# The first gate/up blocks of a decoder layer: scale and shift moved to ScalarE, weight low parts moved to VectorE, another load order, seven conditioning rows moved

## The chip, the cores and the metric

The kernel runs on one core of a Trainium2 chip. The metric is the device time of one execution in microseconds (us), as the median over several runs. The core has five engines with queues of their own: TensorE (PE, with weight loads PEld), VectorE (DVE), ScalarE (ACT), GpSimd (POOL) and SyncE (SP, which issues the DMAs here). An engine takes its instructions strictly in the order of its queue; semaphores tie the queues together.

## The reference

One decoder layer on a sequence of 1024 rows of width 1024: a gated feed-forward net, a token mixer (a convolution branch and a windowed attention branch), a second feed-forward net, a final norm. All is float32. The change lies at the very start, in the first feed-forward net:

```
c_act = silu(c)
mods = c_act @ w_ada + b_ada          # 9 vectors of 1024: sh1, sc1, gt1, sh2, ...
h = rms_norm(x, g_ffn1) * (1 + sc1) + sh1
a, b = split(h @ w1_gu, 2)            # two times 2816 columns
x = x + 0.5 * gt1 * ((silu(a) * b) @ w1_down)
```

## The kernel before

Activations lie transposed: a tile holds 128 features (one of eight blocks `db`) by 512 rows of the sequence (half `h` 0 or 1). Float32 products are made of three matmuls in a rounded format: each operand is split into a high part (a cast) and a low part (the operand minus its high part), and wh·xh, wh·xl and wl·xh are summed in PSUM (`mm3`, L132; three matmuls, L138, L140, L142). A weight block `w1gu[j, i]` (j of 22 output blocks, i the gate or the up half) is loaded as one 128x1024 tile and split by halves of 512 columns (`split`, L105: the cast on ACT, L106; the subtraction, L107, on DVE or, here at the start, on POOL).

A "conditioning row" is one of the 72 blocks of 128 entries of `mods`: `ada_block` (L222) loads 128 rows of `w_ada` transposed and makes 128 dot products with silu(c) in one DVE instruction (L225). For the first norm, the rows m=0 (shift) and m=1 (scale) of each `db` are needed, 16 in all; `ada_done` (L229) turns the scale row into g·(1+sc), `amod`, on DVE (L235).

The first three output blocks (j = 0, 1, 2: six weight tiles, `w0[0]` to `w0[5]`) are worked on while the sixteen rows are still being made, one feature block after another, in an order written out by hand for DVE, ACT, SP and POOL (`manual_schedule`; PE is in hand order everywhere). For half 0: the sum of squares of x (`Stats`, L308: squares on ACT, L312 and L315, adds on DVE, L319; then four matmuls with a column of ones, L328, and a short chain on ACT and DVE, L253 to L260, `rstd`), spread over the partitions by four matmuls (L269) and copied to SBUF (`first_spread`, L640). Then eight times `first_step`, L665: DVE forms u = x·amod·spread (L275), ACT adds the shift and casts to the high part (L279), DVE makes a row of the next block, the low part (L290) and the other row, ACT writes the full value over x (L285). Between the steps stand `first_w` (two casts on ACT, two subtractions on POOL) and `first_mm`, the matmuls of the tiles whose weights are ready. The steps 6 and 7 are followed by the sum of squares of half 1, whose `rstd`, spread and `first_h` start the same work for half 1, with all six tiles ready.

Behind the hand order a planner takes over: it orders the later instructions of DVE, ACT, SP and POOL by its own estimate of times, and it may set a later instruction into the hand-ordered part where it expects an engine to be idle there. First behind the hand order come `all_seven` (sums and differences of the inputs for a seven-product scheme, L179 to L183), the products of blocks 0 to 2, `some_ada(7)` (seven conditioning rows of m=2), and `gu_seven` for the blocks 3 to 21 with one row for each block (`extra`). Weights and rows here go through one ring of four 128x1024 buffers (`load_st`, L112).

Of the kernel before, what the change touches and what calls it, by code (L numbers as in the profile page):

```python
# [10 lines left out]
AF = mybir.ActivationFunctionType  # L11
ALU = mybir.AluOpType

P = 128
# [21 lines left out]
def tile_macaron_layer(  # L36
# [36 lines left out]
    def bank():  # L73
        return ps.tile([P, 512], F32, tag="ps", name=nm("ps"), bufs=8)
# [4 lines left out]
    def tile_t(dt=F32R, shape=(P, 2, HALF)):  # L79
        return act.tile(list(shape), dt, tag="T", name=nm("t"), bufs=28)  # L80
# [4 lines left out]
    def scratch(tag, shape=(P, HALF)):  # L85
        return scr.tile(list(shape), F32, tag="r", name=nm(tag), bufs=8)
# [8 lines left out]
    def f32(t):  # L95
        return t.bitcast(F32)
# [4 lines left out]
    def pair_of(t):  # L101

        return t[:, 0, :], t[:, 1, :]

    def split(hi, lo, src, lo_engine=nc.vector):  # L105
        nc.scalar.copy(hi, src)  # L106
        lo_engine.tensor_tensor(lo, src, f32(hi), op=ALU.subtract)  # L107

    def parts_tile():
        return wgt.tile([P, 2, HALF], F32R, tag="w", name=nm("w"), bufs=8)  # L110

    def load_st(src):  # L112
        st = wgt.tile([P, 1024], F32, tag="wr", name=nm("wr"), bufs=4)
        nc.sync.dma_start(st[:, : src.shape[1]], src)
        return st

    class Weights:


        def __init__(self, raw, n=1024, lo_engine=nc.vector, tiles=None):  # L120
            self.half = m = n // 2
            self.t = tiles or [parts_tile() for _ in range(2)]
            for i in range(2):
                hi, lo = pair_of(self.t[i])
                split(hi[:, :m], lo[:, :m], raw[:, i * m : (i + 1) * m], lo_engine)

        def __call__(self, c0, n=P):
            i, c = c0 // self.half, c0 % self.half
            return self.t[i][:, 0, c : c + n], self.t[i][:, 1, c : c + n]

    def load_w(src, lo_engine=nc.vector, tiles=None):
        return Weights(load_st(src), src.shape[1], lo_engine, tiles)  # L132

    def mm3(outs, w, xs, start, stop):

        wh, wl = w
        for o, (xh, xl) in zip(outs, xs):
            mm(o, wh, xh, start=start, stop=False)  # L138
        for o, (xh, xl) in zip(outs, xs):
            mm(o, wh, xl, start=False, stop=False)  # L140
        for o, (xh, xl) in zip(outs, xs):
            mm(o, wl, xh, start=False, stop=stop)  # L142
# [130 lines left out]
    def modulated_hi(xsrc, pb, which, db, hi):  # L273
        u = scratch("u")
        nc.vector.scalar_tensor_tensor(  # L275
            out=u, in0=xsrc, scalar=amod[:, which * 8 + db : which * 8 + db + 1], in1=pb,
            op0=ALU.mult, op1=ALU.mult,
        )
        nc.scalar.activation(  # L279
            hi, u, AF.Identity, bias=mods[:, which * 24 + db : which * 24 + db + 1]  # L280
        )
        return u

    def modulated_full(u, which, db, dst):
# [193 lines left out]
    def gu_seven(wgu, js, hid, ts, extra=lambda to: None):  # L478

        seven_stream([(wgu[j, 0], wgu[j, 1], GateValue(hid, j)) for j in js], ts, extra)  # L480
# [151 lines left out]
    with tc.tile_pool(name="f1", bufs=2) as tmp:  # L632
# [3 lines left out]
        def load_x(h):  # L636
            for db in range(KT):
                nc.sync.dma_start(xT[db][h], x_block(db, h))

        def first_spread(rr):  # L640
            sp = scratch("spr")
            nc.scalar.copy(sp, spread(rr))
            return sp

        def first_h(dbs, h):
            us = [modulated_hi(xT[db][h], sp, 0, db, hh[db][h]) for db in dbs]
            for u, db in zip(us, dbs):
                modulated_lo(u, 0, db, hh[db][h], hl[db][h])
            for u, db in zip(us, dbs):
                modulated_full(u, 0, db, xT[db][h])  # L650

        def first_ada(db, m):
            ada_block(crow_act, m, db, sta.pop(0))
            if m == 1:
                ada_done(m, db, 1)

        def first_ada_load(db):
            for m in range(2):
                sta.append(tile_c(F32))
                nc.sync.dma_start(sta[-1], wada[m * 8 + db])  # L660

        def first_step(db):

            u = modulated_hi(xT[db][0], sp, 0, db, hh[db][0])
            if db + 1 < KT:  # L665
                first_ada(db + 1, 0)
            modulated_lo(u, 0, db, hh[db][0], hl[db][0])
            modulated_full(u, 0, db, xT[db][0])
            if db + 1 < KT:
                first_ada(db + 1, 1)  # L670

        def first_mm(dbs, h, which):
            for db in dbs:
                for i in which:
                    mm3([first[i, h]], w0[i](db * P),
                        [(hh[db][h], hl[db][h])], db == 0, db == KT - 1)

        def first_w(i):
            w0[i] = Weights(w0[i], 1024, nc.gpsimd, [tile_t(), tile_t()] if i > 3 else None)

        def first_sw(j, h):
            hid.put(j, h, swiglu_raw(first[2 * j, h], first[2 * j + 1, h], h == 0 or None))
# [6 lines left out]
        })  # L689
        order.__enter__()  # L690
        crow_act = tmp.tile([P, D], F32, tag="crow", name="crow_act", bufs=1)
        nc.sync.dma_start(crow_act, crow)
        nc.scalar.activation(crow_act, crow_act, AF.Silu)
        load_x(0)
        s0 = Stats(engine=nc.vector)
        for db in range(KT):
            s0.add(xT[db][0])
        sta, w0 = [], {}
        first_ada_load(0)
        w0[0] = load_st(w1gu[0, 0])  # L700
        w0[1] = load_st(w1gu[0, 1])
        first_ada_load(1)
        w0[2] = load_st(w1gu[1, 0])
        first_ada_load(2)
        w0[3] = load_st(w1gu[1, 1])
        first_ada_load(3)
        first_ada(0, 0)
        r0 = s0.rstd()
        first_ada(0, 1)
        first_w(0)  # L710
        w0[4] = load_st(w1gu[2, 0])
        sp = first_spread(r0)
        first_w(1)
        first = {(i, 0): bank() for i in range(6)}
        first_ada_load(4)
        first_step(0)
        first_mm((0,), 0, (0, 1))
        first_w(2)
        first_ada_load(5)
        first_step(1)  # L720
        first_mm((1,), 0, (0, 1))
        first_mm((0, 1), 0, (2,))
        first_w(3)
        first_ada_load(6)
        first_step(2)
        first_mm((2,), 0, (0, 1, 2))
        first_mm((0, 1, 2), 0, (3,))
        first_w(4)
        first_ada_load(7)
        w0[5] = load_st(w1gu[2, 1])  # L730
        load_x(1)
        first_step(3)
        first_mm((3,), 0, (0, 1, 2, 3))
        first_mm((0, 1, 2, 3), 0, (4,))
        first_step(4)
        first_mm((4,), 0, (0, 1, 2, 3, 4))
        first_step(5)
        first_mm((5,), 0, (0, 1, 2, 3, 4))
        first_w(5)
        s1 = Stats(engine=nc.vector)  # L740
        first_step(6)
        for db in range(2):
            s1.add(xT[db][1])
        first_mm((6,), 0, (0, 1, 2, 3, 4))
        first_step(7)
        for db in range(2, KT):
            s1.add(xT[db][1])
        first_mm((7,), 0, (0, 1, 2, 3, 4))
        r1 = s1.rstd()
        first_sw(0, 0)  # L750
        first_mm((0, 1, 2), 0, (5,))
        sp = first_spread(r1)
        first_mm((3, 4, 5, 6, 7), 0, (5,))
        first.update({(i, 1): bank() for i in range(6)})
        steps = [(m, k) for m in range(2, 9) for k in range(KT)]

        def some_ada(n):
            for _ in range(n):
                if steps:
                    ada_step(crow_act, *steps.pop(0))  # L760
# [11 lines left out]
        ts = all_seven(tt, xT)  # L772
        for j in range(3):
            first_sw(j, 1)
        some_ada(7)
        gu_seven(w1gu, range(3, NJ), hid, ts, lambda to: some_ada(1))

        gate, ngate = gates_of(2)
        xT = by_half(tile_x)
# [626 lines left out]
```

## Time and profile before

| | us |
|---|---|
| median of three runs | 2294.13 (2292.82 to 2300.34) |
| the profiled execution | 2291.84 |
| its span, first to last instruction | 2289.7 |
| PE busy in the span | 2206.0 (96%) |
| DVE busy | 1675.7 (73%) |
| ACT busy | 1061.9 (46%) |
| POOL busy | 395.0 (17%) |

The span is the time between the first and the last instruction on the chip; what lies around it, 2.1 us, is start and end of the program. A row of the timeline gives the start of an instruction, its duration, its engine and line, and in brackets how long the engine had been idle before it and what released it. "x8" is a run of eight instructions of one kind in one row. L269 and L328 show two PE instructions for one matmul of the program. A duration is longer than the distance to the next instruction, since instructions overlap in an engine's pipeline; where instructions follow each other, the distance of the starts is what one costs.

### The profile page before, as it was taken

What the parts mean: (1) busy time and instruction counts of PE and PEld (TensorE: products, weight loads), DVE (VectorE), ACT (ScalarE), POOL (GpSimd) and SP (SyncE); (2) the same over time, 40 slices, a digit from 0 to 9 for tenths busy, and PEclk for the clock granted to TensorE, in tenths of its full rate; (3) what the DMA queues carried; (4) which work ended last, traced back from release to release, by engine and by line L of the source; (5) the groups of instructions that cost most, each with busy time, mean ns of one, the idle gap of its engine ahead of it and who ended that gap; (6) DMA issues with size and microseconds to landing.
All of it is one profiled execution on the core that took longest, in us unless ns stands there. A gap on an engine that the chain in (4) does not pass through costs nothing.

```text
span 2289.7 us, 30099 instructions
## 1 busy us (share of the span) xinstructions
PE 2206.0 (96%) x10392; PEld 1845.3 (81%) x10392; DVE 1675.7 (73%) x2966; ACT 1061.9 (46%) x2095; POOL 395.0 (17%) x445
## 2 busy tenths in 40 slices
PE   5899999999998999999899997999999999999997
PEld 3688888888887888888889996788888888888786
DVE  8897778767868777777477776554786776676876
ACT  4554444444446443343476555123644444454443
POOL 3000000006452000000344443002100000002644
PEclk9899999999999999999999998999999999999998
DMA  8265456599732543444121115454233553389932
GB/s 322 74 221 172 149 185 212 181 406 299 270 115 106 184 134 107 155 157 155 56 64 57 49 48 212 133 170 155 75 120 120 184 184 120 120 326 343 337 116 74
DMA packets 146744, 381.63 MB, mean 167 GB/s; under 512 B 20384, under 2 KB 22560, under 8 KB 146592
## 3 DMA queue, kind: packets, MB, share of 16 engines
q1 hardware_dynamic: 141984, 371.33, 46.5%
q0 software_dynamic: 4608, 8.39, 2.1%
q8 instruction: 81, 1.33, 0.2%
q14 instruction: 71, 0.58, 0.1%
HBM read 270.61 MB, written 109.05 MB: 166 GB/s over the span
## 4 chain that ended last, share of the span: by engine, by line
PE 86%; DVE 7%; issue 2%; ACT 1%; DMA 1%; POOL 1%; SPq 0%; POOLq 0%; DVEq 0%; ACTq 0%
PE ps L195 60%; PE ps L142 6%; PE ps L140 6%; PE ps L138 6%; PE ps L977 2%; PE ps L975 2%; PE ps L976 2%; DVE w L107 1%; PE ps L1031 1%; PE ps L1074 1%; DVE t L225 1%; DMA wr<-in_w2d_dram 1%; POOL s L319 1%; PE ps L1010 1%; PE ps L1098 1%
## 5 line engine op out<-in xcount | busy, mean ns | idle before, releaser
L195 PE MATMUL ps<-t,w 128*128 128x512 f32 x6468 | 1469.2, 389 | 5.0 <-DVE r L405 3.0
L195 PEld LDWEIGHTS ps<-t,w 128*128 128x128 f32 x6468 | 1213.4, 188 | 260.4 <-DVE r L405 5.8
L106 ACT CAST w<-wr 128x512 fp32r<-128x512 f32 (+1 forms) x420 | 255.3, 613 | 481.2 <-PE ps L195 365.3
L107 DVE TENSOR_TENSOR w<-wr,w 128x512 fp32r<-128x512 f32 (+1 forms) x404 | 304.4, 760 | 137.8 <-ACT w L106 136.2
L515 POOL TENSOR_TENSOR x<-x,g 128x512 f32<-128x512 f32 x96 | 145.2, 1526 | 1061.5 <-DMA t<-hs 941.1
L106 ACT CAST w<-ws 128x512 fp32r<-128x512 f32 x231 | 143.9, 623 | 250.3 <-PE ps L195 200.6
L140 PE MATMUL ps<-t,w 128*128 128x512 f32 (+1 forms) x528 | 204.9, 388 | 6.5 <-DVE t L290 6.5
L107 DVE TENSOR_TENSOR w<-ws,w 128x512 fp32r<-128x512 f32 x231 | 161.4, 703 | 39.4 <-ACT w L106 39.0
L138 PE MATMUL ps<-t,w 128*128 128x512 f32 (+1 forms) x400 | 156.2, 390 | 7.2 <-ACT t L279 7.2
L142 PE MATMUL ps<-t,w 128*128 128x512 f32 (+1 forms) x400 | 154.4, 386 | 1.1 <-DVE w L107 1.1
L140 PEld LDWEIGHTS ps<-t,w 128*128 128x128 f32 x528 | 100.4, 190 | 28.4 <-DVE t L290 9.2
L344 DVE TENSOR_TENSOR x<-x,x 128x512 fp32r<-128x512 f32 x161 | 102.8, 687 | 2.9 <-ACT x L343 2.8
L343 ACT CAST x<-x 128x512 fp32r<-128x512 f32 x161 | 88.8, 624 | 20.4 <-DVE x L431 10.2
L225 DVE CUSTOM_DVE_ANT_0 wr<-wr,crow_act,v 128x1024 f32<-128x1024 f32 x56 | 71.7, 1282 | 36.0 <-DMA wr<-in_wada_dram 35.9
L138 PEld LDWEIGHTS ps<-t,w 128*128 128x128 f32 x400 | 76.4, 191 | 23.9 <-ACT t L279 9.8
L569 DVE SCALAR_TENSOR_TENSOR x<-ps,mods,x 128x512 f32<-128x512 f32 (+1 forms) x104 | 72.9, 706 | 23.6 <-PE ps L195 12.9
L107 POOL TENSOR_TENSOR w<-wr,w 128x512 fp32r<-128x512 f32 (+1 forms) x16 | 21.5, 1358 | 397.3 <-ACT w L106 397.3
L142 PEld LDWEIGHTS ps<-t,w 128*128 128x128 f32 x400 | 76.4, 191 | 16.5 <-DVE w L107 1.8
L319 POOL TENSOR_TENSOR s<-s,q 128x512 f32<-128x512 f32 (+1 forms) x48 | 56.8, 1185 | 188.8 <-ACT q L315 187.3
L975 PE MATMUL ps<-w,t 128*128 128x384 f32 x256 | 88.3, 345 | 0.0
L977 PE MATMUL ps<-w,t 128*128 128x384 f32 x256 | 85.7, 335 | 0.0
L976 PE MATMUL ps<-w,t 128*128 128x384 f32 x256 | 85.6, 335 | 0.0
(150 smaller groups left out, 2815.6 us busy)
## 6 DMA issues: line engine op xcount, KB each, us to landing
t<-hs SPq DMA_DIRECT2D x140, 512.0 KB, 9.9
hs<-x SPq DMA_DIRECT2D x277, 256.0 KB, 4.6
wr<-in_wada_dram SPq DMA_DIRECT2D x56, 512.0 KB, 3.8
wr<-in_w1gu_dram SPq DMA_DIRECT2D x44, 512.0 KB, 4.6
wr<-in_w2gu_dram SPq DMA_DIRECT2D x44, 512.0 KB, 3.6
wr<-in_wbcu_dram SPq DMA_DIRECT2D x24, 512.0 KB, 4.1
wr<-in_w1d_dram SPq DMA_DIRECT2D x22, 512.0 KB, 7.5
wr<-in_w2d_dram SPq DMA_DIRECT2D x22, 512.0 KB, 7.5
```

Of the source, the lines that this page charges most:

```text
L106: nc.scalar.copy(hi, src)
L107: lo_engine.tensor_tensor(lo, src, f32(hi), op=ALU.subtract)
L138: mm(o, wh, xh, start=start, stop=False)
L140: mm(o, wh, xl, start=False, stop=False)
L142: mm(o, wl, xh, start=False, stop=stop)
L195: mm(o, a, b, start=first, stop=last, skip_group_check=True)
L225: nc.vector.tensor_tensor_reduce(out=st, in0=st, in1=crow_act, scale=1.0, scalar=v[:, C_BADA + i : C_BADA + i + 1], op0=ALU.mult, op1=ALU. ...
L344: nc.vector.tensor_tensor(f32r(t), t, f32(hi), op=ALU.subtract)
L515: nc.gpsimd.tensor_tensor(dst, dst, r, op=ALU.add)
L975: mm(o[:, :384], xh, wh, start=k == 0, stop=False)
L976: mm(o[:, :384], xh, wl, start=False, stop=False)
L977: mm(o[:, :384], xl, wh, start=False, stop=k == KT - 1)
```

## The change

In the hand-ordered part:

1. x of half 0 is loaded ahead of the broadcast c (`crow`), and silu(c) stands behind the squares of x on ACT.
2. `amod` is now 1+sc, made on ACT. u is x·g·spread and doesn't depend on the conditioning any more. ACT applies scale and shift and writes the high part and the full value, one right behind the other. The low part is the full value minus the high part, a plain subtraction on DVE, behind both rows of the next block.
3. The spread for half 0 is read by DVE from PSUM, without the copy. Twelve small matmuls that nobody reads (`keep_busy`) stand on PE ahead of it, eight behind it.
4. The weight tiles are split half by half (`LateWeights.make`), with the subtraction on DVE in place of POOL, at places listed in `plan`; the matmuls of a step are issued as all high ones (`first_mm_hi`), then all low ones (`first_mm_lo`), then the tiles that are caught up (`late`).
5. The loads of the rows, of x of half 1 and of the last two weight tiles stand at other places of SP's order. The sum of squares of half 1 is spread over the steps 4 to 7.
6. `some_ada(7)` goes; the blocks 10 to 17 of `gu_seven` take two rows each instead of one.

```diff
+        def make(self, i):
+            split(*pair_of(self.t[i]), self.raw[:, i * HALF : (i + 1) * HALF])
...
+        def first_u(db, h):
+            u = scratch("u")
+            nc.vector.scalar_tensor_tensor(
+                out=u, in0=xT[db][h], scalar=v[:, C_G1 + db : C_G1 + db + 1], in1=sp,
+                op0=ALU.mult, op1=ALU.mult,
+            )
+            return u
+        def first_hi(u, db, h):
+            for dst in (hh[db][h], xT[db][h]):
+                nc.scalar.activation(
+                    dst, u, AF.Identity, bias=mods[:, db : db + 1],
+                    scale=amod[:, db : db + 1],
+                )
+        def first_lo(db, h):
+            nc.vector.tensor_tensor(
+                hl[db][h], xT[db][h], f32(hh[db][h]), op=ALU.subtract)
...
         def first_ada(db, m):
             ada_block(crow_act, m, db, sta.pop(0))
             if m == 1:
-                ada_done(m, db, 1)
+                nc.scalar.activation(
+                    amod[:, db : db + 1], mods[:, 8 + db : 9 + db], AF.Identity, bias=ones)
...
+        def keep_busy(n):
+            o = bank()
+            for _ in range(n):
+                mm(o[:, 0:P], ident, ident, start=True, stop=True)
...
+        load_x(0)
         nc.sync.dma_start(crow_act, crow)
-        nc.scalar.activation(crow_act, crow_act, AF.Silu)
-        load_x(0)
         s0 = Stats(engine=nc.vector)
         for db in range(KT):
             s0.add(xT[db][0])
+        nc.scalar.activation(crow_act, crow_act, AF.Silu)
...
         first_ada(0, 0)
+        first_ada(0, 1)
         r0 = s0.rstd()
-        first_ada(0, 1)
...
+        keep_busy(12)
+        first_ada(1, 0)
+        sp = spread(r0)
+        keep_busy(8)
+        first_ada_load(5)
+        load_x(1)
+        first_ada_load(6)
+        first_ada_load(7)
...
+        plan = (
+            ([(0, 0), (1, 0)], (0, 1), ()),
+            ([(2, 0)], (0, 1), [((0, 1), (2,))]),
+            ([(3, 0)], (0, 1, 2), [((0, 1, 2), (3,))]),
+            ([(0, 1), (1, 1)], (0, 1, 2, 3), ()),
+            ([(2, 1)], (0, 1), [((4,), (2,))]),
+            ([(4, 0)], (0, 1, 2), [((0, 1, 2, 3), (4,))]),
+            ([(3, 1)], (0, 1, 2), [((4, 5, 6), (3,))]),
+            ([(4, 1), (5, 0), (5, 1)], (0, 1, 2, 3), [((4, 5, 6, 7), (4,))]),
+        )
+        for db, (pieces, which, late) in enumerate(plan):
+            first_hi(first_u(db, 0), db, 0)
+            for i, part in pieces:
+                if i > 3 and part == 0:
+                    w0[i] = load_st(w1gu[2, i - 4])
+                first_w(i, part)
+            first_mm_hi((db,), 0, which)
+            if db + 1 < KT:
+                if db:
+                    first_ada(db + 1, 0)
+                first_ada(db + 1, 1)
+            first_lo(db, 0)
+            first_mm_lo((db,), 0, which)
+            for dbs, tiles in late:
+                first_mm(dbs, 0, tiles)
+            if db >= 4:
+                for d in (2 * db - 8, 2 * db - 7):
+                    s1.add(xT[d][1])
         r1 = s1.rstd()
         first_sw(0, 0)
-        first_mm((0, 1, 2), 0, (5,))
+        first_mm((0, 1, 2, 3), 0, (5,))
         sp = first_spread(r1)
-        first_mm((3, 4, 5, 6, 7), 0, (5,))
+        first_mm((4, 5, 6, 7), 0, (5,))
...
-        some_ada(7)
-        gu_seven(w1gu, range(3, NJ), hid, ts, lambda to: some_ada(1))
+        gu_seven(w1gu, range(3, NJ), hid, ts,
+                 lambda to: some_ada(1 if to.j < 10 or to.j >= 18 else 2))
```

## Rows read from the trace of the kernel before

**Rows 1.** Busy time of the engines in three stretches of the first 115 us. Columns: stretch, its length, then busy us and instructions of PE, PEld, DVE, ACT, POOL, the granted clock, the DMA share, GB/s.
```profile
20.00:40.00 20.00, 11.73 (x33) 7.80 (x34) 19.71 (x22) 8.08 (x15) 14.10 (x8) 1.00 1.03 407
60.00:80.00 20.00, 11.13 (x40) 8.71 (x39) 16.12 (x30) 6.15 (x11) 0.00 (x0) 0.68 0.55 184
100.00:115.00 15.00, 15.00 (x68) 12.43 (x67) 15.00 (x26) 7.71 (x15) 0.00 (x0) 1.00 0.12 35
```

**Rows 2.** Who waited for whom before 85 us: the waiting engine and line, the releaser, us in total, times, the longest.
```profile
PE ps L328 <- DVE s L319: 21.8, 2, 13.2
PE ps L138 <- ACT t L279: 7.2, 5, 2.4
PE ps L140 <- DVE t L290: 4.7, 6, 2.2
```

**Rows 3.** The timeline of DVE between the last low part and the sum of squares of half 1: the first of the seven rows of m=2, and the last add.
```profile
60.97 1.28 DVE L225 CUSTOM_DVE_ANT_0 wr<-wr,crow_act,v 128x1024 f32<-128x1024 f32 x1
...
72.42 0.69 DVE L319 TENSOR_TENSOR s<-s,q 128x512 f32<-128x512 f32 x1
```

**Rows 4.** The timeline of DVE in the steps: u of the first step, u of the third, one whole step, and a run of plain subtractions later on.
```profile
20.08 0.75 DVE L275 SCALAR_TENSOR_TENSOR u<-x,amod,spr 128x512 f32<-128x512 f32 x1 [0.37 <-ACT spr L642]
...
33.10 1.75 DVE L275 SCALAR_TENSOR_TENSOR u<-x,amod,spr 128x512 f32<-128x512 f32 x1
...
44.15 0.75 DVE L275 SCALAR_TENSOR_TENSOR u<-x,amod,spr 128x512 f32<-128x512 f32 x1
44.82 1.28 DVE L225 CUSTOM_DVE_ANT_0 t<-t,crow_act,v 128x1024 f32<-128x1024 f32 x1
...
46.02 0.75 DVE L290 SCALAR_TENSOR_TENSOR t<-u,mods,t 128x512 fp32r<-128x512 f32 x1
...
48.21 0.75 DVE L275 SCALAR_TENSOR_TENSOR u<-x,amod,spr 128x512 f32<-128x512 f32 x1
...
100.31 1.89 DVE L107 TENSOR_TENSOR t<-x,t 128x512 fp32r<-128x512 f32 x3
```

**Rows 5.** The timeline of ACT: the high part, the full value and two casts in the first step, the high part of the fifth, and the squares of half 1.
```profile
20.98 0.72 ACT L279 ACTIVATE t<-u,mods 128x512 fp32r<-128x512 f32 x1
21.61 0.71 ACT L285 ACTIVATE x<-u,mods 128x512 f32<-128x512 f32 x1
22.22 1.12 ACT L106 CAST w<-wr 128x512 fp32r<-128x512 f32 x2
...
44.94 0.73 ACT L279 ACTIVATE t<-u,mods 128x512 fp32r<-128x512 f32 x1 [2.72 <-DVE u L275]
...
60.78 3.23 ACT L315 ACTIVATE q<-x 128x512 f32<-128x512 f32 x6
```

**Rows 6.** The timeline of PE: the sum of squares and the spread of half 0, the same of half 1 with matmuls of the last tile around them, and the first matmul of half 1.
```profile
13.19 1.87 PE L328 MATMUL ps<-ones,s 128*128 128x1 f32 x8 [13.19 <-DVE s L319]
17.37 2.05 PE L269 MATMUL ps<-ident,nr 128*128 128x128 f32 x8 [2.32 <-DVE nr L260]
...
73.16 1.87 PE L328 MATMUL ps<-ones,s 128*128 128x1 f32 x8 [8.59 <-DVE s L319]
74.89 0.77 PE L138 MATMUL ps<-t,t 128*128 128x512 f32 x1
...
78.87 1.91 PE L269 MATMUL ps<-ident,nr 128*128 128x128 f32 x8
80.44 0.73 PE L138 MATMUL ps<-t,t 128*128 128x512 f32 x1
...
83.99 0.39 PE L142 MATMUL ps<-t,t 128*128 128x512 f32 x1
84.21 0.39 PE L138 MATMUL ps<-t,w 128*128 128x512 f32 x1
```

**Rows 7.** The timeline of ACT at the start, up to the square root of half 0.
```profile
4.79 1.06 ACT L693 ACTIVATE crow_act<-crow_act 128x1024 f32<-128x1024 f32 x1 [2.77 <-DMA crow_act<-in_crow_dram]
...
7.80 3.94 ACT L315 ACTIVATE q<-x 128x512 f32<-128x512 f32 x6 [0.40 <-DMA x<-in_x_dram]
11.75 1.28 ACT L253 ACT_TABLE_LOAD   x1
15.09 0.26 ACT L253 ACTIVATE nt<-ps,eps 128x4 f32<-128x4 f32 x1 [2.05 <-PE ps L328]
```

**Rows 8.** The timeline of PE at idle stretches later in the kernel.
```profile
688.42 1.05 PE L328 MATMUL ps<-ones,s 128*128 128x1 f32 x8 [0.30 <-POOL s L319]
693.43 1.16 PE L269 MATMUL ps<-ident,nr 128*128 128x128 f32 x8 [2.47 <-DVE nr L260]
1402.97 0.80 PE L138 MATMUL ps<-t,t 128*128 128x512 f32 x1 [5.44 <-ACT t L106]
```

**Rows 9.** Busy time of the engines in three stretches of 19 us, about one block of `gu_seven` each; columns as in rows 1.
```profile
269.00:288.00 19.00, 19.00 (x86) 15.73 (x85) 16.26 (x28) 10.41 (x19) 0.00 (x0) 1.00 0.60 201
288.00:307.00 19.00, 19.00 (x86) 15.73 (x85) 17.59 (x30) 10.41 (x19) 0.00 (x0) 1.00 0.79 273
307.00:326.00 19.00, 19.00 (x85) 15.75 (x84) 12.98 (x21) 7.08 (x12) 0.00 (x0) 1.00 0.47 162
```

More of the change, by code (lines that the diff above doesn't have):

```diff
@@ L129, in __call__, with __init__ @@
             return self.t[i][:, 0, c : c + n], self.t[i][:, 1, c : c + n]
+    class LateWeights(Weights):
+        def __init__(self, raw, tiles):
+            self.half, self.raw = HALF, raw
+            self.t = tiles or [parts_tile() for _ in range(2)]
+        def make(self, i):
+            split(*pair_of(self.t[i]), self.raw[:, i * HALF : (i + 1) * HALF])
     def load_w(src, lo_engine=nc.vector, tiles=None):
@@ L643, in first_spread @@
             return sp
+        def first_u(db, h):
[14 more added lines that the diff above has]
+                hl[db][h], xT[db][h], f32(hh[db][h]), op=ALU.subtract)
         def first_h(dbs, h):
-            us = [modulated_hi(xT[db][h], sp, 0, db, hh[db][h]) for db in dbs]
+            us = [first_u(db, h) for db in dbs]
             for u, db in zip(us, dbs):
-                modulated_lo(u, 0, db, hh[db][h], hl[db][h])
-            for u, db in zip(us, dbs):
-                modulated_full(u, 0, db, xT[db][h])
+                first_hi(u, db, h)
+            for db in dbs:
+                first_lo(db, h)
         def first_ada(db, m):
@@ L660, in first_ada_load, with first_mm_hi, first_mm_lo, first_w @@
                 nc.sync.dma_start(sta[-1], wada[m * 8 + db])
[L662 to L670, printed above, removed]
+        def first_mm_hi(dbs, h, which):
+            for db in dbs:
+                for i in which:
+                    wh, wl = w0[i](db * P)
+                    mm(first[i, h], wh, hh[db][h], start=db == 0, stop=False)
+                    mm(first[i, h], wl, hh[db][h], start=False, stop=False)
+        def first_mm_lo(dbs, h, which):
+            for db in dbs:
+                for i in which:
+                    mm(first[i, h], w0[i](db * P)[0], hl[db][h], start=False,
+                       stop=db == KT - 1)
         def first_mm(dbs, h, which):
             for db in dbs:
[L674 to L679, printed above, removed]
+                first_mm_hi((db,), h, which)
+                first_mm_lo((db,), h, which)
+        def keep_busy(n):
+            o = bank()
+            for _ in range(n):
+                mm(o[:, 0:P], ident, ident, start=True, stop=True)
+        def first_w(i, part):
+            if part == 0:
+                w0[i] = LateWeights(w0[i], [tile_t(), tile_t()] if i > 3 else None)
+            w0[i].make(part)
         def first_sw(j, h):
@@ L697, in tile_macaron_layer @@
             s0.add(xT[db][0])
+        nc.scalar.activation(crow_act, crow_act, AF.Silu)
         sta, w0 = [], {}
         first_ada_load(0)
+        first_ada_load(1)
         w0[0] = load_st(w1gu[0, 0])
         w0[1] = load_st(w1gu[0, 1])
-        first_ada_load(1)
+        first_ada_load(2)
         w0[2] = load_st(w1gu[1, 0])
-        first_ada_load(2)
+        first_ada_load(3)
         w0[3] = load_st(w1gu[1, 1])
-        first_ada_load(3)
+        first_ada_load(4)
         first_ada(0, 0)
+        first_ada(0, 1)
@@ L708, in tile_macaron_layer @@
         r0 = s0.rstd()
-        first_ada(0, 1)
[L710 to L713, printed above, removed]
-        first = {(i, 0): bank() for i in range(6)}
[L715 to L739, printed above, removed]
-        s1 = Stats(engine=nc.vector)
-        first_step(6)
-        for db in range(2):
-            s1.add(xT[db][1])
@@ L744, in tile_macaron_layer @@
[L744 to L748, printed above, removed]
+        keep_busy(12)
[6 more added lines that the diff above has]
+        first_ada_load(7)
+        first = {(i, 0): bank() for i in range(6)}
+        s1 = Stats(engine=nc.vector)
+        plan = (
[8 rows of a table added]
+        )
[17 more added lines that the diff above has]
+                    s1.add(xT[d][1])
```

## The prediction, made before the changed kernel was seen

> **What bounds the kernel now.** I read the windows first: from 100 us on PE is busy in all of its time (15.00 of 15 us), while in 60 to 80 us it is busy for 11.13 of 20 and in 20 to 40 us for 11.73 [rows 1]. So whatever the change does to the end, it does by moving the point from which PE runs without a pause. I take as this point the first matmul of half 1, at 84.21 us [rows 6]; from u of the first step, at 20.08 us [rows 4], it is 64.1 us away.
>
> The waits say what holds PE up before: 21.8 us for the sums of squares (L328 for L319), in two waits, then 7.2 us for high parts and 4.7 us for low parts [rows 2]. The second wait for the squares, 8.59 us up to 73.16 [rows 6], is DVE's doing: it makes seven rows of m=2 from 60.97 us on, between the adds, and the last add starts at 72.42 [rows 3]. A row costs 1.20 us (44.82 to 46.02 [rows 4]), so the seven cost 8.4 us, nearly the whole wait. In the steps DVE is the engine that never rests: 19.71 us of 20 [rows 1]. A step without POOL beside it takes 4.06 us (44.15 to 48.21), and u takes 1.75 us in place of 0.75 at 33.10 [rows 4], in the stretch where POOL is busy for 14.10 us [rows 1].
>
> **The change part by part.** I follow DVE from the first u (time 0) to the point above.
>
> *The start (parts 1 to 3).* The squares came 3.94 us for six, paced by the loads, while later six took 3.23 us [rows 7, 5]. With 512 KB of c behind x and not ahead, which is two tiles of x at 0.66 us, the sum of squares on PE (13.19 us before [rows 6]) starts between 0 and 1.3 us earlier; I take 1.3, as the squares waited for loads. Its matmuls take 1.87 us, so PE is at 13.8. The twelve unread matmuls are quarters of a spread, 0.29 us each at PE's high level (1.16 us for four [rows 8]), 0.51 at its low one (2.05 [rows 6]): 3.5 to 6.1 us, and the spread behind them 1.2 to 2.1 us: 18.5 to 22.0 us for u. On the other branch the squares end at 10.4 (1.3 us before 11.74), and ACT then needs a table for silu (1.28 us, as at 11.75), silu (1.06), waits for both rows of block 0 (2.4), makes `amod`, which now stands ahead of the square root, loads its table (1.28) and takes the root (0.26): about 17.0 us. From root to spread it was 2.28 us (15.09 to 17.37 [rows 7, 6]), some of it under POOL: the spread starts at about 19 us. Both branches put u near 20.1 us, where it was: the start is worth 0, bounds -1.6 and +1.9 us. Without the silu table it would be the first branch that decides, at the same time. SP issues x first and c later, the loads behind are the same bytes; DMA share was 1.03 in 20 to 40 us [rows 1] and the rows were never waited for [rows 2], so that order costs nothing; if a load were late, its step would be, 1.3 us for each 512 KB.
>
> *A step (parts 2, 4).* In the queue of DVE a low part of a weight half stands right behind u, and it needs a cast, which on ACT stands behind both activations on that u. So DVE waits. From the rows: ACT starts 0.79 us after u (44.15 to 44.94 [rows 4, 5]); an activation with a bias operand costs 0.63 us (20.98 to 21.61), one without 0.52 (3.23 us for six, the last 0.63 long) [rows 5]. The new ones have a scale operand too, which no row shows: between 0.63 and 0.74 each; I take 0.72. Then the cast, 0.60. The subtraction starts at 0.79 + 2 x 0.72 + 0.60 + 0.05 = 2.9 us of the step, and what stood idle on DVE behind u is 2.2 us. Queued behind it: the other half, the rows of the next block, the low part; PE waits for all of these. The rest: subtraction 0.60 (three in 1.89 us, the last 0.69 long [rows 4]), row 1.20, low part 0.60.
>
> The Trainium skill (ScalarE: Activation LUTs, section What ACT_TABLE_LOAD costs) says that each per-partition pointer operand adds some 93 ns to an activation; the trace agrees for the first one, 0.11 us. By it the second would be 0.72 us, and the sixteen in the steps 1.5 us dearer than the old ones; no run here shows it yet.
>
> - Step 0: 2.9 + two halves 1.2 + one row 1.2 + low 0.6 = 5.9.
> - Steps 1 and 2: 2.9 + 0.6 + 2.4 + 0.6 = 6.5 each. Step 3, with two halves: 7.1.
> - Step 4: rows end at 5.9; behind them ACT makes `amod` (about 0.2) and two squares (0.52 and 0.62), then one add: 8.0. Steps 5 and 6, with two adds that follow each other: 8.2 each.
> - Sum up to step 7: 5.9 + 13.0 + 7.1 + 8.0 + 16.4 = 50.4 us.
> - Step 7: 2.9 + three halves 1.8 + low 0.6 = 5.3; then PE has four low matmuls and twelve late ones ahead of the sum of squares, 16 x 0.227 (0.22 from 83.99 to 84.21 [rows 6]) = 3.6: 9.0 us with gaps. The adds end sooner, at 6.7, and are no bound. Together 59.4 us.
>
> *From there to the point above.* With PE at its high level the sum of squares takes 1.0 us [rows 8], twelve matmuls of tile 5 2.7, which cover root and chain, the spread 1.0, the other twelve 2.7, which cover copy, u and high part: 7.4 us. Before, this was 84.21 - 73.16 = 11.05 us, with nine matmuls 0.44 us apart (74.89 to 78.87) and a spread of 1.91 [rows 6], after the long pause. So 59.4 + 7.4 = 66.8 us against 64.1: **2.7 us later**. What the seven rows (8.4 us) and POOL's collisions (some ten of 1 us) give back, DVE spends on twelve subtractions (7.2 us) and eight waits of 2.2 us.
>
> *Part 6.* Eight more rows in blocks 10 to 17 cost DVE 9.6 us in blocks where it is busy for 16.26, 17.59 and 12.98 us of 19 [rows 9]; PE has no pause there. 17.59 + 1.20 = 18.8 us still fits: 0, with 9.6 as the other end if none did.
>
> **Sum.** The profiled execution is 2291.84 us; 2291.84 + 2.7 = 2294.5. The median of the runs lies 2.3 us above the profiled one: **2296.8 us**. The forecast's own range is -3 to +6 us around no change plus that shift: 2291 to 2302.
>
> **Rivals.**
>
> *A: DVE doesn't wait for the casts (faster).* DVE's own work from the first u is 8 x 0.67 + 12 x 0.60 + 13 x 1.20 + 8 x 0.60 + 7 x 0.60 = 37.2 us. If the wait were hidden, the sum of squares would follow at about 41 us, not 59.4: 18 us better, 16 us faster than before, 2278 us; half of it hidden gives 2287. For it: ACT is busy for only 8.08 us of 20 [rows 1]. Against: ACT's queue is strict, and the order written there is high, full, cast.
>
> *B: PE falls to its low level in the steps (slower).* In each step PE has 4 to 8 high matmuls and then waits for the low part, 3 to 4 us. In the trace PE went on at its high level after an idle time of 2.47 us (a spread of 1.16 us) and was at the low one after 5.44 us (a matmul of 0.80) [rows 8]; the gaps lie between these. Decided by whether the gaps of the last three steps count as rest: their 63 matmuls at 0.44 us take 27.7 us from 35.5 us on, so the sum of squares starts at 63.2 and not 59.4, and what follows costs 11.8 and not 7.4 us: 8.2 us more, about 2305 us. [...] The Trainium skill (TensorE: Matmul & The Clock Gate, section Why this matters for your kernels) warns against idle gaps between bursts of matmuls in just this way; by that rule B is the case, but the row after 2.47 us says that not every gap does it.
>
> *C: The moved rows come back.* If the blocks that make hidden parts are over full, DVE's lateness reaches PE: up to 9.6 us for eight rows, 2306 us with the forecast. For it: 18.8 of 19 us. Against: the next block leaves room (12.98), and weights are prepared a block ahead.
>
> **How the numbers follow.** Forecast 0.58, A 0.18, B 0.17, C 0.07. A measurement of this kernel can tell 0.3%, 6.9 us, from no change. The forecast and the weak forms of all three fall within: 0.58. Faster needs A nearly whole: 0.19. Slower needs B or C nearly whole, or both in part: 0.23. The range reaches down to a bit under half of A and up to B and C: 2283 to 2306.
>
> **What would show it.** Right, if DVE idles about 2.2 us behind each u, released by a cast (L106); if u follows u by about 6.5 us in the first steps and 8 later; if the sum of squares of half 1 starts near 79 us and takes 1.0 us; if the first matmul of half 1 is near 87 us; if no DVE instruction takes 1 us longer than its kind. A shows as u following u by 4 to 5 us. B shows as matmuls 0.43 us apart in the steps. C shows as new waits of PE for DVE between 250 and 402 us. The forecast is wrong if half 1 begins before 80 or after 93 us, or if PE gains or loses more than 3 us behind that point.

## The result, and the profile after

The changed kernel takes 2297.34 us (median of 20 runs, 2295.05 to 2302.58), the kernel before, on the same chip, 2293.17 us (20 runs): a ratio of 1.0016, with a 95% interval of 1.0009 to 1.0024. That is 2 to 5.5 us slower, less than the 0.3% that were called no change. The forecast was 2296.8 us.

The profiled execution of the changed kernel took 2301.57 us, 4.2 us above its median. Its page says, in the same form as before (busy time, share and instructions of each engine):

```profile
PE 2218.0 (96%) x10432; PEld 1853.7 (81%) x10432; DVE 1666.9 (72%) x2970; ACT 1066.1 (46%) x2103; POOL 374.2 (16%) x433
```

POOL works 20.8 us less and DVE 8.8 us less than before; PE shows 40 instructions more (the 20 unread matmuls) and 12 us more, part of it from matmuls at the low level. Such totals don't say why the time stayed where it was; the stretches do.

The windows answer to [rows 1] (columns as there):

```profile
20.00:40.00 20.00, 12.53 (x46) 8.37 (x46) 12.87 (x21) 7.48 (x13) 0.00 (x0) 0.83 1.03 404
40.00:60.00 20.00, 13.05 (x39) 8.26 (x38) 12.73 (x21) 8.24 (x14) 0.00 (x0) 0.77 0.33 112
60.00:80.00 20.00, 14.10 (x47) 10.28 (x48) 14.66 (x24) 8.82 (x16) 0.00 (x0) 0.80 0.18 56
80.00:100.00 20.00, 19.91 (x96) 16.23 (x95) 11.49 (x22) 10.42 (x16) 0.00 (x0) 1.00 0.07 24
```

DVE, which never rested between 20 and 40 us before (19.71 of 20), now idles for 7.1 and 7.3 us of the first two stretches, and yet the stage is longer. POOL, busy for 14.10 us there before, has nothing to do. PE isn't full either. Everyone waits; these of the waits of the first 90 us say for whom (waiting engine and line, releaser, us in total, times, the longest):

```profile
...
PE ps L704 <- DVE t L672: 16.3, 8, 2.9
ACT t L666 <- DVE u L658: 15.7, 9, 3.9
DVE w L107 <- ACT w L106: 12.9, 6, 2.2
PE ps L338 <- DVE s L329: 12.1, 1, 12.1
...
DVE t L107 <- ACT t L106: 4.3, 2, 2.2
```

PE waits for DVE's low parts (L672), ACT for DVE's u (L658), and DVE eight times for a cast of ACT (L106), 12.9 + 4.3 = 17.2 us in all. The 12.1 us of L338 are the start of the kernel; the wait of 8.59 us for the second sum of squares [rows 6] is gone. One step on the timeline of DVE (start, length, what, and in brackets the idle time ahead of it and its releaser) shows the ring closed:

```profile
26.59 0.74 DVE L658 SCALAR_TENSOR_TENSOR u<-x,v,ps 128x512 f32<-128x512 f32 x1
29.48 0.69 DVE L107 TENSOR_TENSOR w<-wr,w 128x512 fp32r<-128x512 f32 x1 [2.15 <-ACT w L106]
30.09 1.28 DVE L235 CUSTOM_DVE_ANT_0 t<-t,crow_act,v 128x1024 f32<-128x1024 f32 x1
...
33.11 0.74 DVE L658 SCALAR_TENSOR_TENSOR u<-x,v,ps 128x512 f32<-128x512 f32 x1
```

and the same stretch on ACT, where the cast stands behind both activations on that u:

```profile
27.43 0.81 ACT L666 ACTIVATE t<-u,mods,amod 128x512 fp32r<-128x512 f32 x1 [1.03 <-DVE u L658]
28.15 0.80 ACT L666 ACTIVATE x<-u,mods,amod 128x512 f32<-128x512 f32 x1
28.85 0.60 ACT L106 CAST w<-wr 128x512 fp32r<-128x512 f32 x1
```

The stage ends as follows on PE (compare [rows 6]): the sum of squares of half 1, the spread, and the first matmul of half 1.

```profile
82.46 0.95 PE L338 MATMUL ps<-ones,s 128*128 128x1 f32 x8
...
86.13 1.05 PE L279 MATMUL ps<-ident,nr 128*128 128x128 f32 x8
...
89.78 0.39 PE L698 MATMUL ps<-t,w 128*128 128x512 f32 x1
```

So half 1 starts 89.78 - 84.21 = 5.6 us later than before. Where the moved rows now stand, PE has no pause: between 250 and 402 us it is busy for 151.98 of 152 us (152.00 before), while DVE works for 124.87 us and not 116.97.

Behind that, the profiled execution lost some 4 us more, at places which the change doesn't touch. The largest is the next pair of sum of squares and spread; first after, then before:

```profile
716.34 1.87 PE L338 MATMUL ps<-ones,s 128*128 128x1 f32 x8 [2.52 <-POOL s L329]
726.02 1.05 PE L279 MATMUL ps<-ident,nr 128*128 128x128 f32 x8
```

```profile
711.11 1.05 PE L328 MATMUL ps<-ones,s 128*128 128x1 f32 x8 [0.81 <-POOL s L319]
717.57 1.05 PE L269 MATMUL ps<-ident,nr 128*128 128x128 f32 x8
```

After a longer idle time PE worked at its low level (1.87 us for the sum of squares in place of 1.05), and the distance from sum to spread grew from 6.46 us to 9.68. The longer idle time alone doesn't decide this, as the last section shows. The medians don't show the loss: they differ by 4.2 us, less than the first stage alone.

### The profile page after: what moved, and what is told of

The parts are those of the page before. It is cut to its first block, busy times and chain, and to the rows that moved or that the text cites. A ratio compares the mean times of both kernels' runs of the same rounds, so it can differ in the third digit from the quotient of the medians.

```text
span 2299.4 us, 30164 instructions
## 1 busy us (share of the span) xinstructions
PE 2218.0 (96%) x10432; PEld 1853.7 (81%) x10432; DVE 1666.9 (72%) x2970; ACT 1066.1 (46%) x2103; POOL 374.2 (16%) x433
## 4 chain that ended last, share of the span: by engine, by line
PE 87%; DVE 5%; DMA 4%; ACT 2%; issue 2%; POOL 1%; SPq 0%; POOLq 0%; DVEq 0%; ACTq 0%
PE ps L205 61%; PE ps L152 5%; PE ps L150 5%; PE ps L148 5%; PE ps L1019 2%; PE ps L1021 2%; PE ps L1020 2%; DVE w L107 1%; PE ps L1075 1%; PE ps L1118 1%; DMA t<-in_wada_dram 1%; DMA wr<-in_w2d_dram 1%; DMA t<-ycv 1%; PE ps L704 1%; PE ps L1054 1%
## 5 line engine op out<-in xcount | busy, mean ns | idle before, releaser
L205 PEld LDWEIGHTS ps<-t,w 128*128 128x128 f32 x6468 | 1214.4, 188 | 261.4 <-DVE r L415 5.1
L106 ACT CAST w<-wr 128x512 fp32r<-128x512 f32 (+1 forms) x420 | 254.8, 612 | 480.7 <-PE ps L205 358.7
L106 ACT CAST w<-ws 128x512 fp32r<-128x512 f32 x231 | 143.5, 621 | 249.6 <-PE ps L205 204.6
L150 PE MATMUL ps<-t,w 128*128 128x512 f32 (+1 forms) x464 | 178.8, 385 | 0.4 <-DVE t L300 0.4
L152 PE MATMUL ps<-t,w 128*128 128x512 f32 (+1 forms) x336 | 128.8, 383 | 2.0 <-DVE w L107 2.0
L148 PE MATMUL ps<-t,w 128*128 128x512 f32 (+1 forms) x336 | 130.2, 387 | 0.0
L150 PEld LDWEIGHTS ps<-t,w 128*128 128x128 f32 x464 | 88.2, 190 | 17.7 <-DVE t L300 0.9
L152 PEld LDWEIGHTS ps<-t,w 128*128 128x128 f32 x336 | 64.1, 191 | 14.6 <-DVE w L107 2.4
L148 PEld LDWEIGHTS ps<-t,w 128*128 128x128 f32 x336 | 64.3, 191 | 11.9
L441 DVE SCALAR_TENSOR_TENSOR x<-ps,r 128x512 f32<-128x512 f32 x47 | 32.5, 691 | 52.4 <-PE ps L205 52.4
```

Source lines behind the costliest of these rows:

```text
L205: mm(o, a, b, start=first, stop=last, skip_group_check=True)
```

## The experiments

The theory behind them: the first stage is paced by the 2.2 us that DVE stands behind each u, because the subtraction at the head of its queue needs a cast that ACT does last. Rivals: DVE's added subtractions cost the time, or PE's level, or the rows. Each kernel's times are set beside the kernel before in the same session, whose medians were 2293.4 to 2293.9 us; the interval of a ratio reaches 2 to 4 us to either side. All kernels compute the whole reference.

**The casts ahead of the activations.** On ACT the cast of a step's weight halves now stands ahead of the two activations on u; on DVE nothing moves.

```diff
         for db, (pieces, which, late) in enumerate(plan):
-            first_hi(first_u(db, 0), db, 0)
             for i, part in pieces:
...
-                first_w(i, part)
+                first_cast(i, part)
+            first_hi(first_u(db, 0), db, 0)
+            for i, part in pieces:
+                w0[i].low(part)
```

> The changed kernel, with the casts of a step's weight halves ahead of the two activations on ACT; nothing else moves. Theory (DVE waits 2.15 us behind each u for a cast that stands behind two activations): the eight waits go, u follows u by about 4.3 us in the first steps, the sum of squares of half 1 starts near 65 us and not at 82.5, and the kernel takes 16 to 18 us less than the changed one, about 2280 us, 0.6% under the kernel before. Rival 1 (DVE's own work or PE is the bound anyway): under 5 us less, and DVE without idle time between the steps. Rival 2 (PE at its low level is what holds the steps): little changes, matmuls stay 0.43 us apart.

Measured: 2280.61 us, a ratio of 0.9944 (0.9932 to 0.9956): 12.8 us faster than before and 16.7 faster than the changed kernel. On DVE the subtraction follows u with no wait (but for 1.47 us in step 5, see "the rest of the waits"), and the next u comes after 4.28 us and not 6.52:

```profile
24.78 0.74 DVE L663 SCALAR_TENSOR_TENSOR u<-x,v,ps 128x512 f32<-128x512 f32 x1
25.44 0.69 DVE L143 TENSOR_TENSOR w<-wr,w 128x512 fp32r<-128x512 f32 x1
...
29.06 0.74 DVE L663 SCALAR_TENSOR_TENSOR u<-x,v,ps 128x512 f32<-128x512 f32 x1
```

Half 1 starts at 74.33 us, 15.5 us sooner than in the changed kernel. What the twelve subtractions cost is the same in both; it is the wait that goes. Both rivals expected little change, and 16.7 us refute them.

**The rows ahead of the subtraction.** The cast stays where the change put it. On DVE the two rows of the next block stand ahead of the subtraction, so that it does something while ACT gets there.

```diff
-                first_w(i, part)
-            first_mm_hi((db,), 0, which)
+                first_cast(i, part)
             if db + 1 < KT:
                 if db:
                     first_ada(db + 1, 0)
                 first_ada(db + 1, 1)
+            for i, part in pieces:
+                w0[i].low(part)
+            first_mm_hi((db,), 0, which)
```

> The changed kernel with the cast where the change put it (ACT: high, full, cast), but on DVE the two rows of the next block ahead of the subtraction of the weight half. Theory, the loss is what stands queued behind the waiting subtraction: the rows now fill the 2.2 us, u follows u by about 4.3 us in steps 1 and 2 as with the casts first, step 0 takes 4.7, only step 7, which has no rows, still waits; sum of squares of half 1 at 65 to 68 us and a time of 2279 to 2283 us. Rival, it is the place of the cast on ACT that costs (PE gets the low part of a tile's half late, beside the low part of the step, and its matmuls pile up): the steps are short but the sum of squares comes at 70 us or later, 2285 us or more.

Measured: 2280.5 us, 0.9947 (0.993 to 0.9963). Same step, same length, other order:

```profile
24.89 0.74 DVE L663 SCALAR_TENSOR_TENSOR u<-x,v,ps 128x512 f32<-128x512 f32 x1
25.55 1.28 DVE L240 CUSTOM_DVE_ANT_0 t<-t,crow_act,v 128x1024 f32<-128x1024 f32 x1
...
27.96 0.69 DVE L143 TENSOR_TENSOR w<-wr,w 128x512 fp32r<-128x512 f32 x1
...
29.16 0.74 DVE L663 SCALAR_TENSOR_TENSOR u<-x,v,ps 128x512 f32<-128x512 f32 x1
```

The sum of squares starts at 64.67 us and half 1 at 71.99. A late cast therefore cost nothing here, as DVE had work ahead of the instruction that needs it; the rival (matmuls piled up behind late parts) is refuted.

**The low parts back on POOL.** One word: the half tiles' subtractions run on GpSimd.

```diff
-            split(*pair_of(self.t[i]), self.raw[:, i * HALF : (i + 1) * HALF])
+            split(*pair_of(self.t[i]), self.raw[:, i * HALF : (i + 1) * HALF], nc.gpsimd)
```

> The changed kernel, with the subtractions of the weight halves on POOL again (part 4 undone in this one place). Theory (the wait behind u is what the move to DVE costs): DVE goes from u straight to the rows, a step has 3.7 us of DVE's work and loses about 1 us for each half that POOL makes beside it, so u follows u by 4.7 to 5.5 us, and the kernel takes 8 to 13 us less than the changed one. Rival (POOL's collisions were the dearer half, so that the move to DVE is worth it): no gain, or slower than the changed kernel.

Measured: 2279.52 us, 0.9944 (0.9931 to 0.9958), 17.8 us less than the changed kernel, where 8 to 13 were expected. u follows u by 3.00 and 6.12 us in the first two steps and by 4.77 and 4.76 in the next two. DVE no longer waits for a cast, but pays for sharing, as before the change: beside POOL a row took 1.65 or 2.27 us and a low part 1.75.

```profile
23.75 1.65 DVE L235 CUSTOM_DVE_ANT_0 t<-t,crow_act,v 128x1024 f32<-128x1024 f32 x1
...
25.33 2.27 DVE L235 CUSTOM_DVE_ANT_0 t<-t,crow_act,v 128x1024 f32<-128x1024 f32 x1
...
27.54 1.75 DVE L672 TENSOR_TENSOR t<-x,t 128x512 fp32r<-128x512 f32 x1
```

Three ways to keep DVE from waiting end within 1.1 us of each other. So, as far as these times can tell, it doesn't matter which engine makes the subtractions once DVE doesn't wait: twelve subtractions of 0.6 us against the collisions. This is not a comparison of the two at their best, as the casts first together with the subtractions on POOL was not run. POOL waits 42.8 us for casts in this run, 20.7 of them at the start; PE waits for POOL twice, 2.1 us in all.

**The rows alone.** The kernel before, with nothing of the change but the move of the seven rows to blocks 10 to 17.

```diff
-        some_ada(7)
-        gu_seven(w1gu, range(3, NJ), hid, ts, lambda to: some_ada(1))
+        gu_seven(w1gu, range(3, NJ), hid, ts,
+                 lambda to: some_ada(1 if to.j < 10 or to.j >= 18 else 2))
```

> The kernel before with part 6 alone: the seven rows of m=2 are made later, two to a block in blocks 10 to 17. Theory: the sum of squares of half 1 starts 6 us earlier, near 67 us, and as PE then rests for only some 2.5 us, the stage behind it may run at the high level, 3 us more: 6 to 9 us less than before, about 2285 us. In the blocks 10 to 17 no new wait of PE. Rival (the rows come back later): within 2 us of before, and PE waits for DVE between 250 and 400 us.

Measured: 2289.0 us, 0.9979 (0.997 to 0.9988), 4.4 us faster, where 6 to 9 were expected. Between 250 and 402 us PE is busy for 152.00 of 152 us, so the rows don't come back later, and the rival is refuted. The first stage did gain 7.2 us, as half 1 starts at 77.00; from the sum of squares to there it took 9.00 us and not 7.32 as in the changed kernel, since PE fell to its low level a little after its idle time. Later matmuls of the last tile stand 0.43 us apart:

```profile
68.00 1.05 PE L328 MATMUL ps<-ones,s 128*128 128x1 f32 x8 [3.00 <-DVE s L319]
...
69.92 0.63 PE L140 MATMUL ps<-t,t 128*128 128x512 f32 x1
70.34 0.63 PE L142 MATMUL ps<-t,t 128*128 128x512 f32 x1
...
72.05 1.66 PE L269 MATMUL ps<-ident,nr 128*128 128x128 f32 x8
```

So the rest of the change costs the first stage 89.78 - 77.00 = 12.8 us, less than its eight waits of 2.15 us (17.2), and the moved rows hide part of it. How large a part depends on what they are added to: by itself the move saves 7.2 us of the stage, and undone in the changed kernel it costs 3.75 (the next two runs).

**The rows brought back, with and without the wait.** Two kernels undo that part alone (the diff above turned round): the changed kernel, and the kernel with the casts first.

> The changed kernel with the seven rows of m=2 made ahead of block 3 again (part 6 undone). Theory (DVE has 2.15 us of idle time behind each u, and a row of 1.2 us fits in): the planner sets some rows into these waits, where they cost nothing, and the others ahead of the adds; 1 to 5 us slower than the changed kernel, 2298 to 2302 us. Rival (rows always cost their full time ahead of the sum of squares): 8 us slower, about 2305 us.

> The kernel with the casts first (which ran at 2280.6 us), with the seven rows made ahead of block 3 again. Theory (now DVE has no idle time behind u, so a row costs what it takes): 6 to 9 us slower than with the casts first, 2287 to 2290 us. Rival (the rows still find idle time, in the waits for squares, for the load of tile 4 and for PE's late matmuls): under 4 us slower.

Measured: 2301.55 us, 1.0038 (1.0024 to 1.0051), about 4 us over the changed kernel; and 2283.82 us, 0.9961 (0.9948 to 0.9973), 3.2 us over the casts first. The first expectation held; the second was missed, and its rival came true. Seven rows cost 7 x 1.2 = 8.4 us of DVE, but only about half of it lands on the stage, in both kernels: counted from u of the first step, half 1 comes 4.3 and 4.2 us later. In the first, three rows stand in the very waits behind u (the others ahead of the adds), and these wait there for their own loads, for 2.29, 1.57 and 0.32 us:

```profile
55.40 0.74 DVE L658 SCALAR_TENSOR_TENSOR u<-x,v,ps 128x512 f32<-128x512 f32 x1
58.42 1.28 DVE L235 CUSTOM_DVE_ANT_0 wr<-wr,crow_act,v 128x1024 f32<-128x1024 f32 x1 [2.29 <-DMA wr<-in_wada_dram]
...
59.63 0.69 DVE L107 TENSOR_TENSOR t<-wr,t 128x512 fp32r<-128x512 f32 x1
```

In the second, u follows u as in the kernel without them except in three steps. Step 5, with one row, took 1.8 us more (9.43 in place of 7.60), but 1.0 us of that is a longer wait for the cast of tile 4 (2.46 us in place of 1.47), since the steps began 1.6 us sooner in this run and the load came only 0.6 us sooner:

```profile
45.56 0.69 DVE L143 TENSOR_TENSOR t<-wr,t 128x512 fp32r<-128x512 f32 x1 [2.46 <-ACT t L139]
```

Two rows in step 6 cost 0.25 us, since they took the place of three sums of a later weight tile that stand there otherwise. Four in the last step, from 62.35 us on, cost 2.0 us and not 4.8, as DVE has no row of the next block to make there and PE still has its late matmuls. Without the longer wait the seven rows cost some 3.2 us, as the medians say.

**The unread matmuls left out.** The 20 matmuls of the identity with itself, whose result nobody reads, are taken out.

```diff
-        keep_busy(12)
...
-        keep_busy(8)
```

> The changed kernel without the twenty unread matmuls. Theory (the first spread is bound by ACT's two table loads and the square root as much as by these matmuls, and PE has room in the steps): the first u starts within 0.7 us of 20.7, the steps are as long as they were, the kernel is within 1.5 us of the changed one. Rival (the high level at the start is needed): 2 to 4 us slower, with steps that PE ends.

Measured: 2299.2 us, 1.0027 (1.0019 to 1.0036), about 2 us over the changed kernel, slightly more than expected and as much as the rival's least. At the start they are worth nothing: u of the first step comes at 20.83 us and not 20.67, since the spread starts sooner (18.74, not 19.13) and takes longer. The 2 us are lost sixty microseconds later, in step 7, where PE is at its low level in this run only:

```profile
78.73 2.07 PE L704 MATMUL ps<-t,w 128*128 128x512 f32 x4 [1.23 <-DVE t L672]
80.61 0.63 PE L698 MATMUL ps<-t,t 128*128 128x512 f32 x1
...
84.62 0.95 PE L338 MATMUL ps<-ones,s 128*128 128x1 f32 x8
```

The same four matmuls took 1.21 us in the changed kernel. That one early burst should set the level so much later was not shown; it may as well be chance of where the low stretches fall.

**c first again.** The load of c and its silu stand ahead of x, as before the change.

```diff
-        load_x(0)
         nc.sync.dma_start(crow_act, crow)
+        nc.scalar.activation(crow_act, crow_act, AF.Silu)
+        load_x(0)
...
-        nc.scalar.activation(crow_act, crow_act, AF.Silu)
```

> The changed kernel with c loaded ahead of x and silu ahead of the squares, as before (part 1 undone). Theory (the start is bound alike by the unread matmuls behind the sum of squares and by the rows, the table load and the square root): u of the first step 0.5 to 1.5 us later than 20.7, the kernel within 2 us of the changed one. Rival (x first gives a real gain): the sum of squares 1 to 2 us later and all of it in the end, 2299 us or more.

Measured: 2297.59 us, 1.0018 (1.0009 to 1.0027), as the changed kernel. The first u comes 1.0 us later (21.71), the sum of squares 1.2 later (83.65); the time doesn't resolve it, and one trace hardly does: the kernels with x first and the unread matmuls in place have their first u anywhere from 19.49 to 21.10 us.

**The rest of the waits.** With the casts first, DVE still waits for a square (0.80 us) and for the load of tile 4 (1.47 us). This kernel sets the squares of half 1 ahead of `amod` on ACT, and has the loads of tiles 4 and 5 three and four steps earlier in the program, into other buffers.

```diff
+            if db in (2, 3):
+                w0[db + 2] = tile_c(F32)
+                nc.sync.dma_start(w0[db + 2], w1gu[2, db - 2])
...
+            if db >= 4:
+                squares = [s1.square(xT[d][1]) for d in (2 * db - 8, 2 * db - 7)]
             first_mm_hi((db,), 0, which)
```

> The kernel with the casts first, and in addition the squares of half 1 ahead of amod on ACT (DVE waited 0.80, 0.28 and 0.47 us at its adds) and the raw weight tiles 4 and 5 loaded two and four steps earlier, into buffers of the other ring (DVE waited 1.47 us for the cast of tile 4). Theory (DVE is the bound of the steps): 2 to 3 us less than with the casts first, about 2278 us, the best so far. Rival (PE's matmuls end the steps): no change.

Measured: 2280.88 us, 0.9945 (0.9932 to 0.9957): no change from the casts first, so the expectation was missed. Half 1 starts at 72.41 us, 1.9 sooner, 0.8 of it by an earlier first u; the times don't show it. The adds no longer wait for squares, but the load of tile 4 came hardly sooner: SP, with rows and x ahead in its queue, issued it at 35.77 us in place of 37.50, its cast waited 3.02 us for it, and DVE 2.14 us for the cast. So half of the edit had no effect, and whether PE would end the steps without this wait stays open.

**All runs together.** First matmul of half 1 against the kernel before (84.21 us), and the difference of the medians:

| kernel | half 1 from | shift, us | median, us |
|---|---|---|---|
| changed | 89.78 | +5.6 | +4.2 |
| casts first | 74.33 | -9.9 | -12.8 |
| rows ahead of the subtraction | 71.99 | -12.2 | -13.4 |
| low parts on POOL | 74.42 | -9.8 | -13.9 |
| rows moved alone | 77.00 | -7.2 | -4.4 |
| rows back, casts first | 76.91 | -7.3 | -9.8 |
| rows back | 93.53 | +9.3 | +7.9 |
| no unread matmuls | 91.94 | +7.7 | +5.8 |
| c first | 90.97 | +6.8 | +3.9 |
| squares and loads early | 72.41 | -11.8 | -12.8 |

The shift of this one point orders the kernels roughly, as the prediction supposed. It doesn't give the median to better than 1 to 4 us: the rows moved alone and the rows back with the casts first start half 1 at the same time, and their medians are over 5 us apart. The traces say where to look. From half 1 to the sum of squares near 690 us all eleven, the kernel before included, take 603.3 to 604.2 us, so the shift is still there 600 us later; from there to the last sum of squares, in a part of the program that no edit touches (though the planner may order it otherwise), they take 1573.3 to 1579.2 us. What makes this scatter was not settled, beyond the level of PE at the second pair above. The kernel with the rows ahead of the subtraction, the one with the casts first and the one with POOL beat both the kernel before and the changed one, and can't be told apart.

## Why the prediction was right, step by step

**The point to watch** held for the 600 us behind it, where all traces agree within 0.9 us, and the table follows it roughly; not for what lies behind 690 us.

**The start**: u at 20.67 us against 20.1. Parts 1 to 3 are worth nothing here, as taken; the order of c and x alone is worth about 1.0 us, eaten by ACT, which loads a table for silu, waits for a row to make `amod`, and loads a table again for the root:

```profile
10.84 1.28 ACT L739 ACT_TABLE_LOAD   x1
...
15.76 0.29 ACT L685 ACTIVATE amod<-mods,ones 128x1 f32<-128x1 f32 x1 [2.57 <-DVE mods L235]
16.07 1.28 ACT L263 ACT_TABLE_LOAD   x1
```

**The wait behind u** was the step that carried the forecast: 2.2 us, eight times, from an ACT queue of two activations of 0.72 us and a cast. It came as 2.15 and 2.16. The 0.72 that no row of before showed is 28.15 - 27.43, so the second operand cost 0.72 - 0.63 = 0.09 us. The Trainium skill (ScalarE: Activation LUTs, section What ACT_TABLE_LOAD costs) gives some 93 ns for each pointer operand. The trace agrees.

**The steps**: forecast 5.9, 6.5, 6.5, 7.1, 8.0, 8.2 and 8.2 us; the distances from u to u were 5.92, 6.52, 6.51, 7.13, 8.01, 8.28 and 10.16, then 9.26 (forecast 9.0) to the sum of squares. One term failed: "Steps 5 and 6, with two adds that follow each other: 8.2 each". Step 6 took 1.9 us more (10.16), because three sums of a weight tile of a later block (L164 to L173) stand among its adds, one of them behind its load:

```profile
70.19 0.69 DVE L164 TENSOR_TENSOR ws<-wr 128x512 f32<-128x512 f32 x1 [0.54 <-DMA wr<-in_w1gu_dram]
70.80 0.69 DVE L329 TENSOR_TENSOR s<-s,q 128x512 f32<-128x512 f32 x1
71.40 0.69 DVE L168 TENSOR_TENSOR ws<-ws,wr 128x512 f32<-128x512 f32 x1
72.00 0.69 DVE L173 TENSOR_TENSOR wr<-wr,wr 128x512 f32<-128x512 f32 x1
...
73.20 0.74 DVE L658 SCALAR_TENSOR_TENSOR u<-x,v,ps 128x512 f32<-128x512 f32 x1
```

I had taken the rows out of the steps and not asked what else would be put into the place: the rows are work that stands in no hand-written order, and so are the sums of the next tiles.

**From the sum of squares to half 1**: 89.78 - 82.46 = 7.32 us against 7.4; and the sum of squares took 0.95, as PE no longer pauses ahead of it.

**The moved rows**: forecast 0, found 0 (151.98 of 152 us); DVE works 7.9 us more there, where the forecast had eight rows of 1.20 us. Rival C is refuted.

**The sum**: +2.7 us forecast for the first stage, +5.6 found: 0.6 from the start, 1.9 from step 6, the rest from small terms; 89.78 us lies inside the 80 to 93 that I had allowed for half 1. The profiled execution missed my 2294.5 by 7.1 us, of which 2.9 are this and 4.2 lie behind the point to watch. That is more than the 3 us that I had named as a sign of being wrong: for this execution it did not hold that the time behind the point stays as it was, and the level of PE at the second pair is 3.2 us of it. The medians moved by 4.2 us, 1.5 more than the 2.7 forecast, and the base was too high: I started from a median of 2294.13 us in three runs, and 20 runs gave 2293.17. The two errors cancel to 0.5 us, so a hit that close is luck. The direction is not, nor are the lengths of the steps, which came within 0.1 us up to step 5.

**Rival A** (DVE doesn't wait, 2278 us) priced what was lost: three kernels that remove the wait, each in another way, take 2279.5 to 2280.6 us.

**Rival B** is half right: its sign was there, beside those of the forecast. PE did fall to its low level in the steps (granted clock 0.77 to 0.83 in the windows above), as matmuls 0.43 us apart show:

```profile
28.89 0.63 PE L699 MATMUL ps<-t,w 128*128 128x512 f32 x1
29.31 0.63 PE L698 MATMUL ps<-t,w 128*128 128x512 f32 x1
...
33.24 0.86 PE L704 MATMUL ps<-t,w 128*128 128x512 f32 x2 [2.88 <-DVE t L672]
```

But in the steps PE then waited 1.30 to 2.88 us for a low part of DVE, so the slower matmuls cost nothing until the last step, where PE is the bound; there it was at its high level again. Nor is this level new: the kernel before also has matmuls 0.43 us apart between 25.35 and 32.65 us. The run without the unread matmuls shows the price where it is not: some 2 us, a quarter of the 8.2 that I gave B. The Trainium skill (TensorE: Matmul & The Clock Gate, section Why this matters for your kernels) warns against idle gaps between bursts of matmuls. The trace agrees in part: the level was low behind the gap of 2.88 us at 33.24 and high behind that of 1.64 us at 78.66 (four matmuls in 1.21 us), and a low level cost time only where PE ends last.

## What to carry to other kernels

When a subtraction moves to an engine whose queue is strict, look at the producer's queue, not only at the price of the instruction: here the same twelve subtractions cost 17 us more or less by whether two activations or a cast came first, or whether the rows stood ahead. Either queue can be mended, and here putting independent work ahead of the waiting instruction was as good as making the producer faster. And a change of several parts can hide a gain: read each part's stretch for itself, as a part that by itself saved 7 us of the first stage and the rest that cost it 13 summed to no change.

## What the runs showed of the hardware

- An idle time of about 2.5 us decided nothing by itself. Ahead of the same sum of squares PE had been idle for 2.51 us in two kernels; with the low parts on POOL it was at its low level behind it, with the casts first and the rows back it was not:

```profile
700.70 1.86 PE L338 MATMUL ps<-ones,s 128*128 128x1 f32 x8 [2.51 <-POOL s L329]
```

```profile
703.46 1.05 PE L343 MATMUL ps<-ones,s 128*128 128x1 f32 x8 [2.51 <-POOL s L334]
```

  With the rows moved alone, the sum of squares still took 1.05 us after 3.00 us, and the fall came 1.9 us later (69.92).
- The price of sharing between DVE and POOL differs from instruction to instruction: with the low parts on POOL, a low part of DVE went from 0.69 to 1.75 us, and two rows that follow each other from 1.28 to 1.65 and to 2.27.
